# Three instead of four plain tiles at the head of each feed-forward, and an ordering between its input's readers and its way down

## The chip, the cores and the metric

One core of a Trainium2 chip. The metric is the device time of one execution in microseconds; the median of three runs is given. TensorE (PE) multiplies, VectorE (DVE) and ScalarE (ACT) do the elementwise work, SyncE (SP) and GpSimd (POOL) issue the transfers.

## The reference, cut to what matters

512 tokens of width 1024 pass two layers (feed-forward, a mixing block, feed-forward), a third hybrid layer with a feed-forward of its own, and a last norm. So there are five feed-forwards, each of this form with an inner width of 2816:

```python
def swiglu_ffn(x, norm, w_gate, w_up, w_down):
    h = rms_norm(x, norm)
    return (jax.nn.silu(h @ w_gate) * (h @ w_up)) @ w_down

x = x + 0.5 * swiglu_ffn(x, ...)        # the last one without the 0.5
```

## The kernel before, in words

Activations lie feature-major: `x[d]` is a 128 x 512 tile, eight of them (KD = 8). Every float32 matrix product is made of three float32r matmuls of a high and a low part (`mm3`), and every operand is split into these parts by `split_late`: ACT copies the high part, DVE subtracts to get the low one.

**A feed-forward** (`ffn`) has 22 inner tiles of 128 features, worked in the chunks `CHUNKS`. For each tile of a chunk gate and up are computed, then the chunk's way down adds to all eight `x[d]`. There are two forms of an inner tile:

- *Plain* (`plain_gate_up`, tiles marked "-"): 8 gate blocks and 8 up blocks, 3 matmuls each, with 512 columns: 48 matmuls. Weights come as two units of 8 blocks. The evacuation (`gate`, `up`, `new_gated`) is four DVE instructions of 128 x 512: `sg<-acc,rbc`, `u<-acc,rbc`, `u<-u,sg`, `yl<-u,yh`.
- *In sums* (`gate_up`, tiles marked "+"): seven products of 4 blocks, 3 matmuls each, with 256 columns: 84 matmuls. The products are made of sums of weight quarters and sums of input quarters. `product` waits until all four groups of the input's sums are there.

**The input's sums** are made once in each feed-forward by the thread `forms`: for j = 0 to 3 it reads `x[j]` and `x[j+4]` (two instructions `xn<-x,cols,rbc`, which need the norm's factor `rbc`), forms four differences (`ts`), and splits them into `bs` and `bt`. `xn` and `ts` have one buffer each, under the tags `vh` and `vl`. Those two buffers are afterwards the ones in which `prepare_sums` splits the summed weights of each tile in sums (`vh<-rawu`, `vl<-rawu,vh`), so the first of these splits comes behind the forms. It serves the third product of the tile (`x3` with `t2`).

**The order** on every engine is fixed while the program is written: threads (`spawn`) have a rank, and a planner with assumed costs writes the ready instruction of the lowest rank first. Evacuations and weight splits have rank 0; `forms` has 0.5. An instruction on an engine waits only for those ahead of it there and for its operands.

**The way down** of a chunk of n tiles goes over `down_order(n)`: d = 0 and 1 with all but the last tile, then their last tile, then d = 2 to 7. It has 8n blocks in n weight units, 24n matmuls of 512 columns. Each finished d is added to `x[d]` by one DVE instruction in `down`, which frees one of the four accumulators of `acc`; d + 4 uses that accumulator next.

`prepare` runs up to two weight items ahead, `slot` bounds the split weights to three buffers.

Of the kernel before, what the change touches and what calls it, by code (L numbers as in the profile page):

```python
# [19 lines left out]
KD = D // P  # L20
NT = S // P
FF = 2816
NF = FF // P
CHUNKS = (4, 4, 4, 4, 3, 3)
IN_SUMS = [f for f, c in enumerate("----++++++++++++++++++") if c == "+"]
DH = 64
NEG = -1e30
EPS = 1e-6
# [241 lines left out]
class Net:  # L270
# [520 lines left out]
        return t  # L791


    def forms(self, own, out):


        n, v_ = S // 2, self.tv
        yield from self.all_done([self.norm])
        for j in range(KD // 2):
            xn = self.fw.tile([P, 2, S], F32, tag="vh", name=self.nm("xn"), bufs=1)  # L800
            ts = self.fw.tile([P, 4, n], F32, tag="vl", name=self.nm("ts"), bufs=1)
            for m in range(2):
                d = j + m * (KD // 2)
                yield from v_.scalar_tensor_tensor(out=xn[:, m], in0=self.x[d], scalar=self.col(own, d), in1=self.rbc,
                                                   op0=ALU.mult, op1=ALU.mult)
            (b11, b12), (b21, b22) = [(xn[:, m, :n], xn[:, m, n:]) for m in range(2)]
            yield from v_.tensor_tensor(out=ts[:, 0], in0=b12, in1=b11, op=ALU.subtract)
            yield from v_.tensor_tensor(out=ts[:, 1], in0=ts[:, 0], in1=b22, op=ALU.subtract)
            yield from v_.tensor_tensor(out=ts[:, 2], in0=b22, in1=b12, op=ALU.subtract)
            yield from v_.scalar_tensor_tensor(out=ts[:, 3], in0=ts[:, 1], scalar=-1.0, in1=b21, op0=ALU.mult,  # L810
                                               op1=ALU.subtract)
            bs = [self.fx.tile([P, 3, n], F32R, tag=f"b{j}{x}", name=self.nm("bs")) for x in "hl"]
            bt = [self.fx.tile([P, 4, n], F32R, tag=f"t{j}{x}", name=self.nm("bt")) for x in "hl"]
            flat = lambda a: a.rearrange("p a c -> p (a c)")
            yield from self.split_late(bs[0][:, 0], bs[1][:, 0], b11)
            yield from self.split_late(flat(bs[0][:, 1:3]), flat(bs[1][:, 1:3]), xn[:, 1])
            yield from self.split_late(flat(bt[0][:, :]), flat(bt[1][:, :]), flat(ts[:, :]))
            for k, name in enumerate(("b11", "b21", "b22")):
                out.setdefault(name, []).append([t[:, k] for t in bs])
            for k, name in enumerate(("t1", "t2", "t3", "t4")):  # L820
                out.setdefault(name, []).append([t[:, k] for t in bt])
# [120 lines left out]
    def ffn(self, wg, wu, wd, l, factor, own, gain):  # L942
        self.end_norm()
        with ExitStack() as ctx:
            self.fy = self.pool(ctx, self.nm("ffny"), max(CHUNKS))
            self.fp = self.pool(ctx, self.nm("ffn"), 2)
            self.fw = self.pool(ctx, self.nm("ffnw"), 1)
            self.fx = self.pool(ctx, self.nm("ffnx"), 1)
            self.fx.tile([P, 8], F32, tag="pad", name=self.nm("pad"))
            self.u_left, self.raw_a, self.sums_end = len(IN_SUMS), [], self.sums_begun + len(IN_SUMS)  # L950
            self.load_u()
            self.load_u()
            self.bforms, self.ups, self.turns, self.pending, self.early = {}, [], [], None, []
            self.ybanks = [self.main_bank() for _ in range(2)]
            self.formed = self.spawn(self.forms(own, self.bforms), 0.5)

            def down(ps, d, last):
                yield from self.tv.scalar_tensor_tensor(out=self.x[d], in0=ps, scalar=factor, in1=self.x[d],
                                                        op0=ALU.mult, op1=ALU.add)
                if last:  # L960
                    self.feed(d, gain)

            f0 = 0
            for n in CHUNKS:
                ys, last = [], f0 + n == NF
                for f in range(f0, f0 + n):
                    ys.append((self.gate_up if f in IN_SUMS else self.plain_gate_up)(wg, wu, l, f, f == f0 + n - 1))
                self.flush()
                if last:
                    self.join(*self.ups)  # L970
                    for b, _ in self.ybanks:
                        self.put_bank(b)
                if last and gain is None:
                    self.last_products(self.fp, wd, l, (f0, n), ys, factor)
                    return
                gen = self.tiles(down_units(wd, l, f0, n))
                if last:
                    self.begin_norm()
                pd = {}
                for d, j in down_order(n):  # L980
                    if j == 0:
                        pd[d] = self.acc()
                    y, t = ys[j]
                    self.join(t)
                    self.mm3(pd[d], next(gen), y, j == 0, j == n - 1)
                    if j == n - 1:
                        self.evac(pd[d], down(pd[d], d, last))
                f0 += n
# [1056 lines left out]
def fm_unit(name, l, c0):  # L2045
    return [(name, l, k * P, c0, P) for k in range(KD)]
# [16 lines left out]
def down_order(n):  # L2063

    return ([(d, j) for d in range(2) for j in range(n - 1)] + [(d, n - 1) for d in range(2)]
            + [(d, j) for d in range(2, KD) for j in range(n)])


def down_units(name, l, f0, n):
    return in_eights([(name, l, (f0 + j) * P, d * P, P) for d, j in down_order(n)])  # L2070
# [26 lines left out]
def weight_plan():  # L2097
# [3 lines left out]
    def ffn(g, u, d, l):  # L2101
        f0 = 0
        for n in CHUNKS:
            for f in range(f0, f0 + n):
                if f in IN_SUMS:
                    plan.append(("s", fm_unit(g, l, f * P) + fm_unit(u, l, f * P)))
                else:
                    plan.extend(fm_units(g, l, f * P) + fm_units(u, l, f * P))
            plan.extend(down_units(d, l, f0, n))
            f0 += n  # L2110

    for l in range(2):
        ffn("ffn1_w_gate", "ffn1_w_up", "ffn1_w_down", l)
        gates, merged = iter(range(KD, 3 * KD)), iter(range(0, KD, 2))

        def fill(kinds):
            for kind in kinds:
                if kind == "p":
                    plan.append(fm_unit("w_in", l, GATES + next(gates) * P))
                else:  # L2120
                    d = next(merged)
                    plan.extend(fm_unit("w_in", l, GATES + j * P) for j in (d, d + 1))
                    plan.extend(branch_units(l, [("a", d), ("a", d + 1)]))

        for cols, n in ((cols_A, FILL_A), (cols_B, FILL_B)):
            for h in range(4):
                plan.extend(tm_units("w_in", l, cols(h)))
                fill(n[h])
        for h2 in range(2):
            plan.extend(tm_units("w_in", l, cols_C(h2)))  # L2130
            plan.extend(fm_unit("w_in", l, C_G + (2 * h2 + c) * P) for c in range(2))
            fill(FILL_C[h2])
        fill(FILL_D)
        plan.extend(branch_units(l, MERGE))
        plan.extend(out_units("w_out", l, 0, KD))
        ffn("ffn2_w_gate", "ffn2_w_up", "ffn2_w_down", l)
# [8 lines left out]
    plan.extend(out_units("w_out_2", 0, 4, 12))  # L2145
    plan.extend(out_units("w_out_2", 0, 0, 4))
    ffn("w_gate_2", "w_up_2", "w_down_2", 0)
    plan.extend(down_units("w_down_2", 0, NF - CHUNKS[-1], CHUNKS[-1]))
    return [x if x[0] == "s" else ("n", x) for x in plan]
# [107 lines left out]
```

## Time and profile before

| | us |
|---|---|
| median of three runs | 3151.79 |
| lowest and highest of them | 3150.3, 3155.45 |
| the profiled execution, its own time | 3151.65 |
| its span, first to last instruction | 3149.9 |
| PE busy in the span | 3124.7 (99%) |
| DVE busy in the span | 2349.7 (75%) |
| ACT busy in the span | 1473.7 (47%) |

The profiled execution spends 1.75 us outside the span that the profile shows. Times in rows are microseconds from the span's start. The busy share is a mean over stages that differ.

### The profile page before, as it was taken

To read this page: it belongs to the slowest core of one execution; us is meant where nothing else is said; L and a number is where in the kernel's file an instruction comes from. 1 tells how busy PE (TensorE), PEld (TensorE's weight loads), DVE (VectorE), ACT (ScalarE), POOL (GpSimd) and SP (SyncE) were. 2 spreads that over 40 slices of the span, in tenths; PEclk is the share of its full clock that TensorE was granted. 3 is DMA by queue.
4 is the path that set the end of the run, shared out by engine and by line. 5 is a ranking of instruction groups with operands and counts; after the bars stand their busy time and mean duration, and the time that the engine had idled before them with its cause. 6 is when DMAs were issued, how large, how long until landed. Compare 5 with 4: busy or idle time off the path is not lost.

```text
span 3149.9 us, 48139 instructions
## 1 busy us (share of the span) xinstructions
PE 3124.7 (99%) x18544; PEld 2762.2 (88%) x18544; DVE 2349.7 (75%) x4380; ACT 1473.7 (47%) x2522; POOL 188.6 (6%) x296
## 2 busy tenths in 40 slices
PE   9999999999999999999999999999999999999998
PEld 7999988988889998999988988888999887779997
DVE  8776878776786778866788876768767977687777
ACT  4443545663344444434445574334434445643443
POOL 0000000000100000000000000100000000000000
PEclk9999999999999999999999999999999999999999
DMA  5656434223536563565443322445564323226653
GB/s 171 161 147 160 130 109 119 96 91 112 177 110 163 152 158 114 144 153 149 140 129 113 104 98 87 158 151 134 151 155 130 119 69 107 87 94 158 160 150 101
DMA packets 142742, 410.64 MB, mean 130 GB/s; under 512 B 22432, under 2 KB 23616, under 8 KB 142512
## 3 DMA queue, kind: packets, MB, share of 16 engines
q1 hardware_dynamic: 106848, 308.44, 31.1%
q0 software_dynamic: 35664, 99.12, 13.4%
q8 instruction: 146, 2.39, 0.3%
q14 instruction: 84, 0.69, 0.1%
HBM read 386.47 MB, written 26.21 MB: 131 GB/s over the span
## 4 chain that ended last, share of the span: by engine, by line
PE 97%; DVE 2%; ACT 1%; issue 0%; DMA 0%; SPq 0%; DVEq 0%; ACTq 0%
PE acc L412 80%; PE b L412 15%; PE b L441 2%; DVE wl L204 0%; DVE x L204 0%; DMA raw<-in_wst_dram 0%; DVE o L204 0%; DVE li L204 0%; DVE xgl L204 0%; DVE gl L204 0%; ACT xgh L204 0%; ACT p L204 0%; ACT wh L204 0%; ACT li L204 0%; DVE xc L204 0%
## 5 line engine op out<-in xcount | busy, mean ns | idle before, releaser
L204 DVE TENSOR_TENSOR wl<-raw,wh 128x1024 fp32r<-128x1024 f32 (+2 forms) x465 | 549.4, 1182 | 208.9 <-ACT wh L204 205.9
L204 ACT CAST wh<-raw 128x1024 fp32r<-128x1024 f32 (+2 forms) x465 | 472.7, 1017 | 438.9 <-PE acc L412 269.0
L412 PE MATMUL acc<-xgh,wh 128*128 128x512 f32 x992 | 397.4, 401 | 2.5 <-ACT xgh L204 2.3
L412 PE MATMUL acc<-xgl,wh 128*128 128x512 f32 x992 | 388.4, 392 | 0.9 <-DVE xgl L204 0.8
L412 PE MATMUL acc<-xgh,wl 128*128 128x512 f32 x992 | 388.7, 392 | 0.0
L412 PE MATMUL acc<-yl,wh 128*128 128x512 f32 (+1 forms) x968 | 367.6, 385 | 0.4 <-DVE yl L204 0.3
L412 PE MATMUL acc<-yh,wh 128*128 128x512 f32 (+1 forms) x904 | 347.4, 384 | 0.5 <-ACT yh L204 0.4
L412 PE MATMUL acc<-yh,wl 128*128 128x512 f32 (+1 forms) x904 | 346.8, 384 | 0.0
L412 PE MATMUL acc<-bt,wh 128*128 128x256 f32 x1440 | 260.5, 279 | 0.0
L412 PE MATMUL acc<-wh,xgh 128*128 128x384 f32 (+1 forms) x672 | 248.0, 369 | 0.0
L412 PE MATMUL acc<-wh,xgl 128*128 128x384 f32 (+1 forms) x672 | 234.8, 349 | 0.0
L412 PE MATMUL acc<-wl,xgh 128*128 128x384 f32 (+1 forms) x672 | 234.5, 349 | 0.0
L412 PEld LDWEIGHTS acc<-xgh,wh 128*128 128x128 f32 x992 | 187.4, 189 | 42.8 <-ACT xgh L204 3.8
L204 DVE SCALAR_TENSOR_TENSOR x<-acc,x 128x512 f32<-128x512 f32 (+2 forms) x250 | 165.6, 669 | 75.9 <-PE acc L412 75.8
L412 PEld LDWEIGHTS acc<-xgh,wl 128*128 128x128 f32 x992 | 186.9, 188 | 39.9
L412 PEld LDWEIGHTS acc<-xgl,wh 128*128 128x128 f32 x992 | 187.4, 189 | 39.1 <-DVE xgl L204 2.5
L412 PEld LDWEIGHTS acc<-bt,wh 128*128 128x128 f32 x1440 | 219.4, 188 | 0.0
L412 PEld LDWEIGHTS acc<-yl,wh 128*128 128x128 f32 x968 | 181.2, 188 | 36.0 <-DVE yl L204 1.0
L204 ACT CAST vh<-rawu 128x1024 fp32r<-128x1024 f32 x90 | 94.5, 1050 | 252.7 <-DVE rawu L204 252.7
L412 PE MATMUL acc<-bt,wl 128*128 128x256 f32 x720 | 200.7, 279 | 0.0
L412 PEld LDWEIGHTS acc<-yh,wl 128*128 128x128 f32 x904 | 169.9, 188 | 33.7
L412 PEld LDWEIGHTS acc<-yh,wh 128*128 128x128 f32 x904 | 169.9, 188 | 33.4 <-ACT yh L204 0.6
(325 smaller groups left out, 6812.8 us busy)
## 6 DMA issues: line engine op xcount, KB each, us to landing
raw<-in_wst_dram SPq DMA_DIRECT2D x398, 512.0 KB, 3.3
rawu<-in_wst_dram SPq DMA_DIRECT2D x90, 512.0 KB, 3.7
raw<-in_wst_dram POOLq DMA_DIRECT2D x90, 512.0 KB, 6.2
raw<-in_wst_dram SPq DMA_DIRECT2D x64, 384.0 KB, 3.1
rawa<-in_wst_dram SPq DMA_DIRECT2D x90, 256.0 KB, 4.3
gpark<-gl POOLq DMA_DIRECT2D x48, 256.0 KB, 3.9
mb<-gpark POOLq DMA_DIRECT2D x48, 256.0 KB, 3.6
xpark<-x POOLq DMA_DIRECT2D x24, 256.0 KB, 2.7
```

The lines of the kernel that those rows point to most:

```text
L204: return f(*a, **k)
L412: self.nc.tensor.matmul(out, lhsT, rhs, start=start, stop=stop, **k)
L441: self.nc.tensor.transpose(out, in_, ident)
```

## The change

The first chunk of every feed-forward has three tiles instead of four, and they are all plain; the fourth tile becomes one in sums, the first tile of the second chunk. So 19 of 22 tiles are in sums, where it was 18. The last chunk keeps three tiles, and the third one of the middle gets a fourth.

`forms` now notes in a list, `taken`, when it has read the pair `x[j]`, `x[j+4]`; `down` for d writes its instruction only when the pair of d has been read. This is an order of writing the program: `down` for d stands behind the reading of d's pair on DVE. No semaphore wait is added for it, but what waits for `x[d]` or for the accumulator waits for that place in the order.

```diff
-CHUNKS = (4, 4, 4, 4, 3, 3)
-IN_SUMS = [f for f, c in enumerate("----++++++++++++++++++") if c == "+"]
+CHUNKS = (3, 4, 4, 4, 4, 3)
+IN_SUMS = [f for f, c in enumerate("---+++++++++++++++++++") if c == "+"]
...
-    def forms(self, own, out):
+    def forms(self, taken, own, out):
...
+            taken.append(j)
             (b11, b12), (b21, b22) = [(xn[:, m, :n], xn[:, m, n:]) for m in range(2)]
...
-            self.formed = self.spawn(self.forms(own, self.bforms), 0.5)
+            taken = []
+            self.formed = self.spawn(self.forms(taken, own, self.bforms), 0.5)
 
             def down(ps, d, last):
+                if len(taken) <= d % (KD // 2):
+                    yield lambda: len(taken) > d % (KD // 2)
                 yield from self.tv.scalar_tensor_tensor(out=self.x[d], in0=ps, scalar=factor, in1=self.x[d],
```

## Rows read from the trace of the kernel before

**Rows 1.** The page: the span, the engines' totals, the chain by engine.
```profile
span 3149.9 us, 48139 instructions
...
PE 3124.7 (99%) x18544; PEld 2762.2 (88%) x18544; DVE 2349.7 (75%) x4380; ACT 1473.7 (47%) x2522; POOL 188.6 (6%) x296
...
PE 97%; DVE 2%; ACT 1%; issue 0%; DMA 0%; SPq 0%; DVEq 0%; ACTq 0%
```
**Rows 2.** Windows of plain tiles, of four in sums: length, busy (count) by engine, clock.
```profile
1249.00:1279.40 30.40, 30.40 (x135) 25.16 (x134) 29.63 (x47) 15.08 (x21) 0.00 (x0) 1.00 0.30 96
79.75:119.23 39.48, 39.48 (x336) 39.21 (x336) 30.95 (x42) 20.64 (x34) 0.84 (x1) 1.00 0.56 165
```
**Rows 3.** Timeline of PE: first matmuls of these stages.
```profile
1248.81 0.39 PE L412 MATMUL acc<-xgh,wh 128*128 128x512 f32 x1
1279.41 0.39 PE L412 MATMUL acc<-yh,wh 128*128 128x512 f32 x1
79.58 0.40 PE L412 MATMUL acc<-bs,wh 128*128 128x256 f32 x2
119.24 0.39 PE L412 MATMUL acc<-yh,wh 128*128 128x512 f32 x1
```
**Rows 4.** Windows of five feed-forwards, rbc to the first vl's end; columns as before.
```profile
34.38:81.89 47.51, 47.27 (x218) 39.19 (x217) 46.61 (x73) 23.01 (x31) 2.57 (x3) 1.00 0.52 124
901.28:958.51 57.23, 57.23 (x258) 47.55 (x257) 48.90 (x74) 24.97 (x33) 2.59 (x3) 1.00 0.48 123
1249.01:1302.27 53.26, 53.26 (x241) 44.28 (x240) 47.54 (x73) 24.01 (x32) 2.56 (x3) 1.00 0.50 123
2122.92:2180.09 57.17, 57.17 (x257) 47.47 (x256) 48.84 (x74) 24.91 (x33) 2.59 (x3) 1.00 0.48 123
2801.88:2854.13 52.25, 52.23 (x235) 43.06 (x234) 47.27 (x73) 24.01 (x32) 2.59 (x3) 1.00 0.49 124
```
**Rows 5.** Timeline of DVE, second feed-forward: the fourth plain tile's share.
```profile
931.29 0.68 DVE L204 TENSOR_TENSOR sg<-acc,rbc 128x512 f32<-128x512 f32 x1
931.89 1.21 DVE L204 TENSOR_TENSOR wl<-raw,wh 128x1024 fp32r<-128x1024 f32 x1
933.02 0.74 DVE L204 SCALAR_TENSOR_TENSOR xn<-x,cols,rbc 128x512 f32<-128x512 f32 x1
...
936.09 0.68 DVE L204 TENSOR_TENSOR u<-acc,rbc 128x512 f32<-128x512 f32 x1
936.81 0.69 DVE L204 TENSOR_TENSOR u<-u,sg 128x512 f32<-128x512 f32 x1
937.42 1.22 DVE L204 TENSOR_TENSOR wl<-raw,wh 128x1024 fp32r<-128x1024 f32 x1
938.55 0.68 DVE L204 TENSOR_TENSOR yl<-u,yh 128x512 fp32r<-128x512 f32 x1
```
**Rows 6.** Timeline of PE: first sums product, then first use of vl.
```profile
957.52 0.28 PE L412 MATMUL acc<-bs,wh 128*128 128x256 f32 x1
960.55 0.28 PE L412 MATMUL acc<-bt,vl 128*128 128x256 f32 x1
...
82.75 0.28 PE L412 MATMUL acc<-bt,vl 128*128 128x256 f32 x1
1301.17 0.40 PE L412 MATMUL acc<-bs,wh 128*128 128x256 f32 x2
2179.16 0.40 PE L412 MATMUL acc<-bs,wh 128*128 128x256 f32 x2
2853.03 0.40 PE L412 MATMUL acc<-bs,wh 128*128 128x256 f32 x2
```
**Rows 7.** Timeline of DVE, second feed-forward: the last addition to x.
```profile
960.16 0.68 DVE L204 SCALAR_TENSOR_TENSOR x<-acc,x 128x512 f32<-128x512 f32 x1
```
**Rows 8.** Windows around a fall of the granted clock (seventh column).
```profile
2631.00:2634.60 3.60, 1.37 (x7) 0.84 (x6) 3.52 (x6) 1.25 (x2) 0.00 (x0) 1.00 0.30 101
2634.60:2638.00 3.40, 3.40 (x10) 2.63 (x9) 1.52 (x3) 1.04 (x1) 0.00 (x0) 0.50 0.12 49
```

## The prediction

> **What bounds it now.** I read the page first: PE is busy for 99% of the span and holds 97% of the chain that ended last, while DVE is busy 75% on average [rows 1]. So fewer PE cycles are worth their time, as long as nothing else becomes the last to arrive. An average can't say that, so I then looked at the stretch the change touches, the head of each of the five feed-forwards.
>
> That stretch has one late customer. The first tile in sums needs all forms, and its third product needs `vl`, which DVE writes behind the forms. So I asked for the windows from the writing of `rbc` (before it no form can start) to the end of the first `vl` [rows 4]. In the first feed-forward DVE is busy 46.61 of 47.51 us: it idles 0.90 us and `vl` ends at 81.89, just ahead of its use at 82.75 [rows 6]. The other four windows leave DVE 5.0 to 8.3 us of idle time. PE works on without a break in all five. So the head of a feed-forward is a race between PE's plain tiles and DVE's forms that is nearly even already, and the 75% hides it.
>
> **What it takes from PE.** Plain: 135 matmuls of 512 columns [rows 2] from 1248.81 to 1279.41 [rows 3], so 30.60 / 135 = 0.2267 us each; a tile of 48 is 10.88 us. In sums: 336 matmuls [rows 2] from 79.58 to 119.24 [rows 3], 39.66 / 336 = 0.1180 us each; a tile of 84 is 9.91 us. The difference is 0.97 us, in five feed-forwards **4.8 us**. The blocks of the way down stay the same in number. What the tile in sums adds elsewhere lies behind PE: over four such tiles DVE is busy 30.95 of 39.48 us, ACT 20.64, POOL 0.84 [rows 2]; without that cover DVE has 2.1 us per tile left. Five more accumulating loads on POOL are five times 0.84 us on an engine otherwise idle there.
>
> The Trainium skill, page "TensorE: Matmul & The Clock Gate", section "Back-to-back issue gap", gives columns / 2.4 ns plus 2.5 ns: 215.8 and 109.2 ns here. By it the tiles are 10.36 and 9.17 us and the gain would be 5.9 us. The rows say 226.7 and 118.0 ns, and the measurement decides.
>
> **What it takes from DVE's time.** The first tile in sums comes earlier by a plain tile (10.88 us) and by 24 matmuls of the way down (24 x 0.2267 = 5.44): **16.32 us** in each feed-forward. `rbc` comes no earlier, since the first plain tile starts when it did.
>
> DVE is spared less. The fourth plain tile's share, from start to start [rows 5]: sg 0.60, wl 1.13, u 0.72, u times sg 0.61, wl 1.13, yl some 0.60; with one weight unit of the way down, 1.13, it is **5.9 us**. The forms themselves, the eight additions to x and the weights of the first tile in sums remain, and all but the last additions are needed before `vl`.
>
> So the new end of `vl` is the start of the window, plus DVE's busy time there [rows 4], less 5.9, plus idle that can't be avoided. For that I take 0.9 us, what the first feed-forward keeps under a full backlog. In the other four one addition to x stood behind `vl`, as in the second [rows 7]; PE now stands until all are through, so 0.6 more. PE asks for `vl` 3.03 us after the first product (957.52 to 960.55 [rows 6]), now 16.32 us earlier:
>
> - First: 34.38 + 46.61 - 5.9 + 0.9 = 75.99; asked at 82.75 - 16.32 = 66.43: late by 9.5.
> - Second: 901.28 + 48.90 - 5.9 + 1.5 = 945.78; asked at 944.23: 1.5.
> - Third: 1249.01 + 47.54 - 5.9 + 1.5 = 1292.15; asked at 1301.17 + 3.03 - 16.32 = 1287.88: 4.3.
> - Fourth: 2122.92 + 48.84 - 5.9 + 1.5 = 2167.36; asked at 2179.16 + 3.03 - 16.32 = 2165.87: 1.5.
> - Fifth: 2801.88 + 47.27 - 5.9 + 1.5 = 2844.75; asked at 2853.03 + 3.03 - 16.32 = 2839.74: 5.0.
>
> Together **21.8 us** of PE standing. Bounds: below, up to four additions to x (0.6 us each) could slip behind `vl`, which takes 2.4 us from each and nothing below zero: 7.1 + 1.9 + 2.6 = 11.6 us are left. Above, DVE's old idle stays where it is, and each feed-forward is late by nearly 16.3 - 5.9 = 10.4 less some slack, 9.5 as in the first: 47.5. I stay near the middle sum, because the old idle lies behind the end of the forms, where DVE waited for PE's next accumulator; with forms still to do it has work then.
>
> **The new wait and the last y.** `down` for d = 3 may now stand only behind the fourth pair's reading. What queues behind it is accumulator 3, and with it PE's d = 7, and all the tiles behind. This moves part of PE's standing from the tile in sums into the way down. It adds nothing to DVE's work, so nothing to the sum. Likewise the last plain tile's y: from u to the end of yl is 936.09 to 939.23, 3.1 us [rows 5]; the cover in `down_order` shrinks from 18 to 12 matmuls, 4.1 to 2.7 us. That is 0.4 to 0.8 us of standing in each, ahead of the same late `vl`, and so within its lateness. If `vl` were in time, these five would cost 2 to 4 us alone.
>
> **The clock.** Where PE was busy only 1.37 of 3.60 us, the granted clock in the next 3.40 us was 0.50, half of 2.4 GHz, although PE was busy for all of them [rows 8]: 1.7 us lost. The three long stands (9.5, 5.0, 4.3) can each bring that. Three times 1.7 is 5.1; part falls into the wait itself, so I take **4 us**, with 0 below and twice 5.1 above.
>
> [...]
>
> **Sum.** On the profiled execution's own 3151.65 us (span 3149.9 and 1.75 around it; the median 3151.79 differs by 0.14): - 4.8 + 21.8 + 4 = + 21.0, so **3172.7 us**, 0.7% slower.
>
> **Rivals.**
> - *The cover holds* (the other side): forms arrive in time, only PE's saving shows: 3151.65 - 4.8 = 3146.9, or up to 3150 with the late last y. For it: DVE's 75%, and ACT idle for half of the windows [rows 4]. It decides if DVE can bring `vl` within 66.43 - 34.38 = 32.1 us of `rbc` in the first feed-forward; the work counted is 40.7. Against it: each term of that work has its consumer before `vl`. 8 in 100.
> - *Only the first pays*: the idle of the others takes up all of the delay. - 4.8 + 9.5 + 1.7 = + 6.4, 3158; with additions slipped behind, 3156. The second and fourth windows are within 1.5 us of it, the third and fifth are not. 10 in 100.
> - *Idle stays*: DVE goes on waiting for PE between forms, as the planner's order has it. Half of it kept is 27.4 us of idle in the last four windows [rows 4] less four times 0.9, halved: + 11.9, so 3184.6; all of it with three full clock losses or more, 3200. Beyond 3187: 6 in 100.
> - *The wait stands on top*: d = 7 waits for the fourth pair and PE loses that beside the lateness of `vl`. The two end on the same queue, so I count it inside the forecast; its price would be up to 5 us in the first feed-forward, 3178.
>
> **Range and chances.** The forecast with its bounds, 3158 to 3187, has 76 in 100. Taking in part of the second rival, the range is 3155 to 3187. A difference of 0.2%, 6.3 us, is about what a measurement of this kernel tells from none: from 3145.5 to 3158.1 is "same". The cover holding is counted faster by over 0.2% for part only, since its own 3146.9 is within that bound; 4 in 100 there, 4 to "same", which with the second rival has 14. Slower 82.
>
> **What would show it.** Right: in the first feed-forward DVE has no gap from `rbc` to `vl`; PE has breaks in the first way down and before the first two or three products in sums, ended by DVE's `bs`, `bt`, `vl` or x, some 9.5 us together, 4 to 5 in the third and fifth, 1 to 2 in the second and fourth; the granted clock shows halves behind the long ones; everything behind the first tile in sums keeps its pitch. Wrong: PE unbroken there (cover holds), breaks of 10 us in all five with DVE idle (idle stays), or breaks at weights and transfers, of which this argument has none.

## The result

| | before | after |
|---|---|---|
| median of six runs, us | 3151.25 | 3171.01 |
| lowest and highest, us | 3149.54, 3155.45 | 3168.99, 3172.64 |
| ratio, with its 95% interval | | 1.0052 [1.0043, 1.0062] |
| the profiled execution: time, span, us | 3151.65, 3149.9 | 3172.64, 3170.9 |

The change makes the kernel 0.5 to 0.6% slower. 3172.7 was forecast, from 3155 to 3187. The cost has three sizes here: 16 us by the ratio (14 to 20 by its interval), 19.8 by the medians of the six runs, whose quotient of 1.0063 lies just above that interval, and 21.0 by the two profiled executions. The profiled one of after is the slowest of its six, so what the traces add up to is at the upper end.

The page of the kernel after, the lines that answer to [rows 1]: span, busy time, and the chain that ended last.

```profile
span 3170.9 us, 48597 instructions
PE 3130.4 (99%) x18724; PEld 2771.8 (87%) x18724; DVE 2366.6 (75%) x4405; ACT 1483.0 (47%) x2547; POOL 192.4 (6%) x301
...
PE 91%; DVE 6%; ACT 1%; issue 1%; DMA 0%; SPq 0%; DVEq 0%; ACTq 0%
```

The busy shares say nothing: 99% and 75%, as before. The chain does: DVE's part rose from 2% to 6%. The windows from `rbc` to the end of the first `vl`, one for each feed-forward, answer to [rows 4]; the columns are length, then busy time by engine, then granted clock, DMA share and GB/s.

```profile
34.73:76.46 41.73, 35.28 (x152) 27.92 (x150) 40.73 (x66) 19.50 (x28) 3.42 (x4) 0.90 0.47 120
911.47:955.42 43.95, 43.38 (x203) 35.94 (x201) 42.42 (x67) 20.67 (x29) 3.43 (x4) 1.00 0.50 127
1259.42:1303.30 43.88, 40.41 (x185) 32.77 (x183) 42.02 (x67) 19.95 (x28) 3.41 (x4) 1.00 0.53 123
2137.24:2181.21 43.97, 43.39 (x203) 35.95 (x201) 42.43 (x67) 20.68 (x29) 3.42 (x4) 1.00 0.48 126
2816.97:2859.50 42.53, 39.35 (x179) 32.14 (x177) 41.67 (x67) 20.35 (x29) 3.42 (x4) 0.97 0.53 130
```

All five are alike now. DVE (third busy figure) leaves 0.9 to 1.9 us idle; before, the last four left 5.0 to 8.3. PE (first) is the one with gaps, 6.5 us in the first. The timeline of PE and DVE at the first `vl` answers to [rows 6]: PE takes `vl` 0.05 to 0.06 us behind its end in every feed-forward.

```profile
75.23 1.23 DVE L204 TENSOR_TENSOR vl<-rawu,vh 128x1024 fp32r<-128x1024 f32 x1
76.51 0.58 PE L412 MATMUL acc<-bt,vl 128*128 128x256 f32 x1
...
955.48 0.38 PE L412 MATMUL acc<-bt,vl 128*128 128x256 f32 x1
1303.36 0.39 PE L412 MATMUL acc<-bt,vl 128*128 128x256 f32 x1 [0.35 <-DVE vl L204]
2181.26 0.38 PE L412 MATMUL acc<-bt,vl 128*128 128x256 f32 x1
2859.56 0.58 PE L412 MATMUL acc<-bt,vl 128*128 128x256 f32 x1
```

Each of these, counted from its `rbc`, less the place where the prediction had PE ask for it (66.43 - 34.38 = 32.05 in the first, and so on), is the lateness. "Whole loss" goes on to the first matmul of the second way down: in the first feed-forward it came 79.37 us behind `rbc`, and 84.87 before the change; 79.37 - (84.87 - 16.32) = 10.8.

| feed-forward | forecast late, us | late, us | whole loss, us |
|---|---|---|---|
| first | 9.5 | 41.78 - 32.05 = 9.7 | 10.8 |
| second | 1.5 | 44.01 - 42.95 = 1.1 | 1.1 |
| third | 4.3 | 43.94 - 38.87 = 5.1 | 4.9 |
| fourth | 1.5 | 44.02 - 42.95 = 1.1 | 1.5 |
| fifth | 5.0 | 42.59 - 37.86 = 4.7 | 6.8 |
| together | 21.8 | 21.7 | 25.1 |

The rest of the kernel keeps its pace. From each `rbc` to the next (the last to the end) it takes 9.8, 0.2, 3.9, 0.8 and 5.9 us more than before; the whole loss less a tile's 0.97 is 9.8, 0.1, 4.0, 0.5 and 5.8.

Where PE stands in the first one, in its timeline at the first product in sums (in brackets: idle before it, and what ended that):

```profile
65.09 0.47 PE L412 MATMUL acc<-bs,wh 128*128 128x256 f32 x2 [0.25 <-ACT bs L204]
...
66.79 0.38 PE L412 MATMUL acc<-bs,wh 128*128 128x256 f32 x1 [0.65 <-DVE bs L204]
...
70.23 0.58 PE L412 MATMUL acc<-bs,wh 128*128 128x256 f32 x1 [2.94 <-ACT bs L204]
...
72.85 0.58 PE L412 MATMUL acc<-bs,wh 128*128 128x256 f32 x1 [2.04 <-DVE bs L204]
```

It waits for the third group's and then the fourth group's `bs`. The waiting of `product` for all four groups is thus one of writing the program: on the chip PE begins with the first group's sums and stands inside the product. From 70.23 its matmuls take 0.58 instead of 0.28. The windows of the two stretches with a granted clock (seventh column) of one half, as in [rows 8]:

```profile
68.44:78.66 10.22, 6.39 (x27) 5.92 (x28) 9.62 (x15) 5.12 (x8) 0.00 (x0) 0.50 0.30 67
2857.13:2863.93 6.80, 6.29 (x28) 5.70 (x27) 4.43 (x5) 2.52 (x5) 0.00 (x0) 0.50 0.71 182
```

The whole loss exceeds the lateness by 1.1 us in the first and 2.1 in the fifth. That fits the part of these stretches that lies behind the first use of `vl`: 78.66 - 76.51 = 2.15 us and 2863.93 - 2859.56 = 4.37, half of which is lost. What is slow ahead of it falls into the wait. In the third the clock held.

### The profile page after: what moved, and what is told of

Its sections match the earlier page's. It is cut to its first block, busy times and chain, and to the rows that moved or that the text cites. A ratio compares the mean times of both kernels' runs of the same rounds, so it can differ in the third digit from the quotient of the medians.

```text
span 3170.9 us, 48597 instructions
## 1 busy us (share of the span) xinstructions
PE 3130.4 (99%) x18724; PEld 2771.8 (87%) x18724; DVE 2366.6 (75%) x4405; ACT 1483.0 (47%) x2547; POOL 192.4 (6%) x301
## 4 chain that ended last, share of the span: by engine, by line
PE 91%; DVE 6%; ACT 1%; issue 1%; DMA 0%; SPq 0%; DVEq 0%; ACTq 0%
PE acc L412 74%; PE b L412 15%; PE b L441 2%; DVE wl L204 1%; DVE ts L204 1%; DVE x L204 1%; DVE xn L204 1%; DVE u L204 0%; DVE bt L204 0%; DVE yl L204 0%; DVE sg L204 0%; DMA x<-in_xT_dram 0%; DVE bs L204 0%; ACT wh L204 0%; DVE o L204 0%
## 5 line engine op out<-in xcount | busy, mean ns | idle before, releaser
L412 PE MATMUL acc<-xgh,wh 128*128 128x512 f32 x912 | 366.2, 402 | 3.2 <-ACT xgh L204 2.9
L412 PE MATMUL acc<-xgl,wh 128*128 128x512 f32 x912 | 357.8, 392 | 1.1 <-DVE xgl L204 1.1
L412 PE MATMUL acc<-xgh,wl 128*128 128x512 f32 x912 | 357.6, 392 | 0.0
L412 PE MATMUL acc<-bt,wh 128*128 128x256 f32 x1520 | 277.3, 280 | 0.8 <-DVE bt L204 0.7
L412 PEld LDWEIGHTS acc<-bt,wh 128*128 128x128 f32 x1520 | 232.9, 189 | 1.5 <-DVE bt L204 1.2
L412 PE MATMUL acc<-bt,wl 128*128 128x256 f32 x760 | 212.8, 280 | 0.0
L412 PEld LDWEIGHTS acc<-xgh,wh 128*128 128x128 f32 x912 | 172.2, 189 | 40.4 <-ACT xgh L204 4.4
L412 PEld LDWEIGHTS acc<-xgh,wl 128*128 128x128 f32 x912 | 172.2, 189 | 36.8
L412 PEld LDWEIGHTS acc<-xgl,wh 128*128 128x128 f32 x912 | 172.4, 189 | 36.1 <-DVE xgl L204 2.6
```

The source lines that it names most:

```text
L412: self.nc.tensor.matmul(out, lhsT, rhs, start=start, stop=stop, **k)
```

## The experiments

**The ordering alone.** The kernel before with `taken` in `forms` and `down`, chunks unchanged.

> The kernel before with the ordering in down alone; chunks and forms of the tiles as before. Theory (VectorE's work between rbc and the first vl decides, the ordering adds none): 3151 us, within 1.5 us of before; in the first feed-forward two VectorE instructions change places. Rival (the ordering itself holds the way down and costs): 3 to 5 us more, with TensorE standing in the first way down.

3152.02 us, ratio 0.9995 [0.9986, 1.0004]. The first use of `vl` came 48.39, 59.28, 55.19, 59.28 and 54.19 us behind `rbc`, as before to within 0.03. The ordering costs nothing there.

**The change without the ordering.**

```diff
-                if len(taken) <= d % (KD // 2):
-                    yield lambda: len(taken) > d % (KD // 2)
```

> The kernel after without the ordering in down, so that some additions to x may be written ahead of the forms' reading and the forms then read the added value: this changes the computed numbers and no instruction's amount of work. Theory (the ordering moves additions within VectorE's order and adds nothing): vl ends within 1 us of after, 3170 to 3171. Rival (the ordering holds accumulators and costs on top): 5 us less or more, 3165.

3173.28 us, 1.0059 [1.0042, 1.0076]. In the first feed-forward `vl` was used 75.95 - 33.49 = 42.46 us behind `rbc`, 0.7 later than with the ordering; the second way down began 79.19 behind `rbc`, 0.2 earlier.

```profile
74.42 1.23 DVE L204 TENSOR_TENSOR vl<-rawu,vh 128x1024 fp32r<-128x1024 f32 x1
75.95 0.33 PE L412 MATMUL acc<-bt,vl 128*128 128x256 f32 x1
```

So the wait that the change adds is no part of its cost, to within such tenths, in either kernel.

**The shorter first chunk with 18 in sums.** `CHUNKS` of after, `IN_SUMS` of before.

> Chunks of the kernel after (3, 4, 4, 4, 4, 3) and the ordering, but 18 tiles in sums: the fourth plain tile opens the second chunk. The first tile in sums comes 24 matmuls of the way down earlier, 5.44 us, and VectorE is spared one weight unit, 1.13. Theory: vl is late by 81.89 - 1.13 - (82.75 - 5.44) = 3.5 us in the first feed-forward, in time in the other four; the last y of the three-tile chunk stands 0.85 us in each of these four (as in the profile after): together some 7 us, 3158. Rival (a nineteenth tile in sums is what costs): 3151, as before. Rival (the shorter first chunk is all that costs): 3171.

3166.78 us, 1.0036 [1.0022, 1.0049]: 11 us by the ratio, 7 to 15 by its interval, where 7 were expected. In the first feed-forward `vl` was used at 80.18, 46.56 behind `rbc` and 46.56 - (48.37 - 5.44) = 3.6 late, as forecast, but not for `vl` alone: that ended at 79.30, and what PE waited for last was ACT's copy of an accumulator (`u`).

```profile
79.83 0.51 PE L412 MATMUL acc<-bt,vh 128*128 128x256 f32 x2 [2.73 <-ACT u L204]
```

In the other four PE stood only for y: 0.8 to 0.9 us at `yl`, and 0.65 at `yh` in the third. (These stands are counted from start to start, less a matmul's 0.23; the brackets of the rows show some 0.2 to 0.3 less.) The rest lies elsewhere. In this execution the clock fell to half in the first and second mixing blocks, three times:

```profile
725.40:732.00 6.60, 6.60 (x17) 4.87 (x18) 5.98 (x22) 1.53 (x2) 0.54 (x1) 0.50 0.33 119
790.30:797.00 6.70, 6.70 (x18) 4.87 (x17) 5.96 (x21) 2.00 (x4) 0.55 (x1) 0.50 0.79 297
1957.70:1961.00 3.30, 3.30 (x9) 2.62 (x9) 2.98 (x11) 1.19 (x2) 0.54 (x1) 0.50 0.19 79
```

16.6 us at half are 8.3 lost, an estimate that takes TensorE for the bound there. The profiled executions differ by 18.3 us, so 10 are left, 3 more than expected, and where these lie stays open. Its five executions run from 3161.25 to 3169.94, with a mean granted clock of 0.997 in the shortest and 0.993 in the longest; where it falls, only the profiled one, the longest, shows.

**One tile fewer in sums, chunks of before.** `"-----+++++++++++++++++"`.

> The kernel before with 17 tiles in sums: the fifth tile, first of the second chunk, is plain. Theory: the price of a tile by the pitches, 10.88 - 9.91 = 0.97 us in each of five feed-forwards, 4.8 us more, 3156, with no new standing, since the first tile in sums comes a plain tile later. Rival (a tile in sums saves TensorE nothing once its preparations count): 3151. Rival (VectorE was late in the kernel before too, so more room gains): 3150 or less.

3160.5 us, 1.0019 [1.001, 1.0028], 6 us with 3 to 9 in the interval: 4.8 is in it. From one `rbc` to the next the trace shows it more closely: 867.94, 348.81, 875.08 us against 866.90, 347.73, 873.91 before, 1.0 to 1.2 each (0.97 expected). The fourth pitch is 1.0 shorter, 677.96 against 678.96; there the kernel before has two falls of the clock (the one of [rows 8] and one at 2760.9) that this execution has not. The price of a tile holds, and more room gains nothing.

**Less for DVE.** The low parts of `bs` and `bt` are copied by ACT, where DVE subtracted.

```diff
...
-            yield from self.split_late(flat(bt[0][:, :]), flat(bt[1][:, :]), flat(ts[:, :]))
...
+                yield from self.ta.copy(hi, src)
+                yield from self.ta.copy(lo, src)
```

> The kernel after, but the low parts of the input's sums are copied by ScalarE and not subtracted by VectorE, so the low part holds the whole value: this changes the computed numbers and takes 0.94 + 1.14 = 2.1 us of VectorE's work from each of four groups, 8.3 us from each feed-forward, nothing else. Theory: vl is late by 9.75 - 8.3 = some 1.5 us in the first feed-forward and in time in the others; the last y goes on standing 0.5 to 0.9 in each; so 3151.3 - 4.8 + 1.5 + 4 = 3152, clock unbroken. Rival (transfers, the ordering or the matmuls' own cost): stays at 3168 to 3171.

3161.92 us, 1.0025 [1.0014, 1.0036]. By the ratios 16 us of loss became 8, where 1 was expected. The first window:

```profile
32.62:69.95 37.33, 33.31 (x152) 26.65 (x150) 32.76 (x54) 25.50 (x39) 3.42 (x4) 1.00 0.56 134
```

DVE is busy 8.0 us less than after (40.73), as planned, but the window shrank by 4.4: DVE now idles 4.6 us in turns with ACT, and PE's last wait there is for ACT.

```profile
69.52 0.50 PE L412 MATMUL acc<-bt,vh 128*128 128x256 f32 x2 [1.23 <-ACT u L204]
```

In the second, third and fourth, ACT's copies held back y: 1.15 us at `yh` beside 0.5 at `yl`, where the kernel after stood 0.85 at `yl` in the second and fourth. The whole losses went from 10.8, 1.1, 4.9, 1.5 and 6.8 to 6.9, 1.5, 1.7, 1.8 and 0.8 us. A miss in size, since the edit gave ACT work that arrives last in its turn; the direction is the theory's.

**More for DVE, in both kernels.** `bt`'s low part is written twice, 4.56 us of DVE in each feed-forward.

```diff
+            yield from v_.tensor_tensor(out=flat(bt[1][:, :]), in0=flat(ts[:, :]), in1=flat(bt[0][:, :]).bitcast(F32),
+                                        op=ALU.subtract)
```

> The kernel after in which VectorE writes the low part of each group's bt a second time with the same values: 1.14 us more for VectorE a group, 4.56 us a feed-forward. Theory (VectorE's work from rbc to vl ends last in all five feed-forwards): vl ends 4.5 us later in each, 22.8 us in all: 3194, some more if the granted clock falls in more of them. Rival (only the first is bound by VectorE, the others by y or by PE's own order): some 5 us more, 3176.

> The same second writing in the kernel before: the same 4.56 us of VectorE a feed-forward. Theory: the first feed-forward had 0.8 us of slack at vl and pays 3.8; third and fifth take it up in 5.7 and 5.0 us of idle time less 0.9, second and fourth in 8.3: 3155.5. Rival (VectorE's work costs wherever it stands): 22.8 us, 3174.

In the kernel before, with no ordering, the delay lets additions to x overtake the fourth pair's reading in the first feed-forward (two at 76.44, the reading at 77.64): its forms then have other values, the amount of work is the same.

After: 3204.87 us, 1.0152 [1.0138, 1.0166]. The windows are longer by 4.7, 4.6, 3.7, 4.6 and 5.5 us, 23.1 together, expected 22.8; by the ratios it is 31 us, and this execution has nine stretches at half clock between its first microseconds and its last, three of them, 20.5 us, in mixing blocks:

```profile
33.21:79.59 46.38, 35.68 (x152) 28.03 (x150) 45.35 (x70) 19.65 (x28) 3.42 (x4) 0.89 0.45 108
917.81:966.37 48.56, 44.23 (x203) 36.08 (x201) 47.68 (x72) 21.28 (x30) 3.43 (x4) 1.00 0.51 125
1271.50:1319.12 47.62, 42.10 (x185) 34.43 (x183) 46.58 (x71) 20.82 (x29) 3.41 (x4) 0.92 0.50 116
2160.45:2209.05 48.60, 44.27 (x203) 36.07 (x201) 47.68 (x72) 21.28 (x30) 3.42 (x4) 1.00 0.49 125
2844.20:2892.25 48.05, 40.80 (x179) 33.21 (x177) 46.48 (x71) 20.62 (x29) 3.42 (x4) 0.93 0.46 115
```

Before: 3157.1 us, 1.0011 [1.0002, 1.002], some 3.5 us. The first feed-forward's `vl` is used 85.97 - 33.12 = 52.85 behind `rbc`, 4.5 late (3.8 expected); in the other four no matmul waits for it and PE has no gap. The first three windows:

```profile
33.12:85.92 52.80, 48.69 (x224) 40.02 (x222) 51.62 (x77) 23.89 (x33) 3.42 (x4) 1.00 0.54 123
905.96:963.29 57.33, 57.33 (x259) 47.63 (x258) 52.76 (x78) 24.56 (x33) 2.59 (x3) 1.00 0.48 123
1253.70:1306.48 52.78, 52.78 (x237) 43.80 (x236) 52.04 (x77) 24.10 (x32) 2.56 (x3) 1.00 0.49 122
```

DVE's idle time took it up: 8.3 us became 4.6 in the second, 5.7 became 0.7 in the third. This is the clearest test. The same 4.56 us of DVE is paid in one place of five before, and in all five after.

**Three d to open the first way down.** `down_order(n, 3)` for the first chunk, so that 18 matmuls cover the last y again.

> The kernel after with the way down of the first chunk opened by three d instead of two, so 18 matmuls cover the last plain tile's y as before the change. Theory (vl ends last in all five): the standing at yl, 0.5 to 0.9 us in each, goes, and as much appears at the forms or at vl: within 1 us of after, 3170 to 3171. Rival (the last y is a cost of its own): 4 to 5 us less than after, 3166.

3172.57 us, 1.0055 [1.0041, 1.007]: no gain. The waits of PE in the second feed-forward's way down and first tile in sums (us in total, times, longest): after had 0.6 at `yl`; now

```profile
PE acc L412 <- DVE vl L204: 0.6, 1, 0.6
PE acc L412 <- DVE bt L204: 0.3, 1, 0.3
```

The row of after:

```profile
938.89 0.50 PE L412 MATMUL acc<-yl,wh 128*128 128x512 f32 x1 [0.57 <-DVE yl L204]
```

The late y was cover for the late `vl`, as the forecast had it.

**Matmuls to fill the standing.** 12 ahead of the third and 24 ahead of the fourth block of the first product, into an accumulator that is written anew behind them, in the first, third and fifth feed-forward.

> The kernel after with 36 matmuls of 256 columns, results unused, between the blocks of the first product in sums of the first, third and fifth feed-forward, 36 x 0.118 = 4.2 us inside the standing of 9.7, 5.1 and 4.7 us. vl ends as in after. If the fall of the granted clock there is a cost of its own (in the profile after 1.1 us in the first, 2.1 in the fifth), part of these 3.2 us comes back: 3168 to 3170. If it is not, or the matmuls in between do not hold the clock: 3171, or up to 1 us more where they outlast the standing.

3172.17 us, 1.0049 [1.0037, 1.0062]: no change in all. The windows at the first (two), at the fifth, and in the first mixing block:

```profile
67.10:70.30 3.20, 3.20 (x17) 3.20 (x17) 3.17 (x6) 1.03 (x2) 0.00 (x0) 0.50 0.68 133
70.50:78.60 8.10, 7.96 (x67) 7.75 (x67) 6.62 (x10) 4.68 (x7) 0.00 (x0) 1.00 0.28 73
2858.00:2866.00 8.00, 8.00 (x70) 7.89 (x69) 6.02 (x8) 4.09 (x6) 0.00 (x0) 1.00 0.62 155
729.30:736.00 6.70, 6.70 (x17) 5.08 (x17) 5.67 (x20) 2.28 (x4) 0.54 (x1) 0.50 0.31 117
```

The half clock at the first shrank from 10.2 to 3.4 us, at the fifth it went, and from `rbc` to the second way down they took 0.8 and 2.1 us less; the third took 1.0 more, since 4.2 us of filling there run past the wait. So at the first and the fifth it was PE's standing that brought the fall. And the clock fell in the first mixing block (729), 3.4 us: more than was won.

**Three differences on GpSimd**, to spare DVE in earnest.

```diff
-            yield from v_.tensor_tensor(out=ts[:, 0], in0=b12, in1=b11, op=ALU.subtract)
+            yield from self.tp.tensor_tensor(out=ts[:, 0], in0=b12, in1=b11, op=ALU.subtract)
...
```

> The kernel after with three of the four differences of each group (ts) computed by GpSimd. VectorE is spared 0.45 + 0.35 + 0.34 = 1.1 us a group, 4.5 us a feed-forward. Theory (VectorE's work decides): vl is late by 9.75 - 4.5 = 5.2 us in the first feed-forward, in time in the others, where the last y's 0.9 stays; with the losses of the profile after (10.8, 5.0, 6.8 in first, third, fifth) some 11 us less than after: 3160. If GpSimd's differences are slow, up to 4 us of that are not seen. Rival (transfers, ordering): 3171.

3219.73 us, 1.0205 [1.0188, 1.0223]: 48 us slower than the change, not 11 faster. The first difference on POOL and DVE's next step:

```profile
46.84 0.86 POOL L227 DMA_DIRECT2D raw<-in_wst_dram  x1 [1.97 <-DMA raw<-in_wst_dram]
47.50 1.05 POOL L206 TENSOR_TENSOR ts<-xn 128x256 f32<-128x256 f32 x1
...
49.31 0.72 POOL L206 TENSOR_TENSOR ts<-xn 128x256 f32<-128x256 f32 x1
49.39 0.93 DVE L206 SCALAR_TENSOR_TENSOR ts<-ts,xn 128x256 f32<-128x256 f32 x1 [5.74 <-POOL ts L206]
```

POOL's differences stand behind an accumulating load, which waited 1.97 us for the transfer it adds to; DVE stands 5.74 us for load and differences, and everything behind it on DVE, y included: PE waited 4 to 9 us at `yh` in each feed-forward. The difference itself takes 0.72 to 1.73 us on POOL, 0.42 on DVE. DVE's own fourth difference, 0.42 in after, takes 0.93 to 0.95 in the 16 groups of 20 in which one of POOL's runs beside it for some 0.65 us, and 0.41 in the other four. The Trainium skill, page "GPSIMD Engine Reference", section "3.1 Elementwise — side-by-side cycle accounting", measures a two-operand instruction at 1.96 times DVE's time; the trace has 1.7 to 4.1 times, for a shorter one.

**The first feed-forward as it was, the others with three plain tiles**, three-headed, differences on GpSimd in all five.

> The first feed-forward as before the change (four plain tiles, 18 in sums, chunks of before), the other four with three plain tiles, the three-headed first way down and three differences on GpSimd. Theory: no lateness is left (4.3 and 5.0 less 4.5 in third and fifth, none in the others), so the gain of the tiles shows: 4 x 0.97 = 3.9 less some 0.5 to 1: 3148, 0.1% below before. Rival (GpSimd's chain is slower than VectorE's backlog): 3152 to 3156.

3210.14 us, 1.0176 [1.0159, 1.0192]. GpSimd's cost again, in the first feed-forward too, where most of PE's waiting was for additions to x:

```profile
PE acc L416 <- DVE x L207: 5.5, 4, 2.8
```

No version here beats the kernel before.

## Why the prediction was right

- **Price of the tile in sums, 0.97 us**: held, by the pitches and by the run with 17.
- **The shift of 16.32 us and DVE's 5.9 us less**: held; DVE's busy time fell by 5.9, 6.5, 5.5, 6.4 and 5.6 us. The ends of `vl` were computed at 41.6, 44.5, 43.1, 44.4 and 42.9 us behind `rbc`; measured 41.73, 43.95, 43.88, 43.97 and 42.53. The doubled `bt` shows that DVE's work decides it in all five.
- **Old idle is filled**: held; 0.9 to 1.9 us are left, for which 0.9 was assumed. The 0.6 us for an eighth addition to x ahead of `vl` is right in the third and fifth; in the second and fourth that addition still stood behind `vl` (at 957.08 in the second), and the lateness is 0.4 less than computed.
- **The ordering adds nothing to the sum**: held. But the standing that was to move into the way down, at d = 7, is not there: PE stood in the first way down for `yl` alone, 0.5 us, and its long waits came at `bs`. With the doubled `bt`, PE did stand there in the first feed-forward for an addition to x, 1.1 us.
- **The last y**: 0.5 to 0.9 us as computed, not additive in the second and fourth, as the three-headed order shows. In the third y's high part came late as well, 1.0 us more, which the forecast had not.
- **The clock, 4 us**: the term was somewhat large. It was 1.1 and 2.1 us in two places, with none in the third. The Trainium skill, page "TensorE: Matmul & The Clock Gate", section "HAM oscillation — how this bites in real kernels", tells of a kernel whose PE fell back to half clock at every one of its waits for a transfer. Here two of the five stands brought it, 10.22 and 6.80 us of 0.50.

By the trace the sum is - 4.8 + 25.1 = + 20.3, and `rbc` of the first feed-forward lay 0.35 later in this execution; the spans differ by 21.0.

The mechanism is the one that was forecast. That the numbers meet so closely is in part luck: the five latenesses miss by - 0.4 to + 0.8 us, and the misses cancel to 0.1, and the forecast's + 21.0 meets the profiled execution of after, the slowest of six, while by the ratio it is above the interval. The upper end of the range, 3187, was chosen and not added up; the bounds of the terms would have reached about 3205.

## What to carry to other kernels

An engine at 75% can be the bound of the one stretch that a change shortens: ask what must be done between the earliest moment it can begin and the first use, and compare that with the work of the other engine which covers it. Here PE gave up 16.3 us of cover to save 0.97. Doubling one small instruction of the suspected engine in both kernels tells in one pair of runs where it is the last to arrive. A wait that shows up ahead of a later one need not be a cost: it was removed, and the later one took its place.

## What was not expected of the hardware

The clock falls in the mixing blocks in some executions, without PE standing long: in the run with the shorter chunk it was 0.50 for 6.60 us from 725.4, although PE was busy all of that and in all of the 10.3 us before.

```profile
715.00:725.30 10.30, 10.30 (x57) 8.69 (x55) 4.60 (x11) 3.85 (x8) 0.54 (x1) 1.00 0.23 78
```

In the profiled executions of before and after it held there. What makes it fall stays open. The runs of the kernel before spread over the study from 3149.5 to 3161.3 us, and this spread goes with their mean granted clock: beside the experiments, the 8 runs at 0.997 took 3151.2 us on average, the 12 at 0.995 3154.7, the 4 at 0.993 3158.6. That the clock fell in the mixing blocks in the longer ones is likely but not shown, since none of them was profiled.
